# A two-layer hybrid decoder trunk: x loaded first, rotary angles and gate rows on GpSimd, six first-layer weight tiles stored split, split tiles brought back on two rings

## The chip, the cores and the metric

The kernel runs on one core of a Trainium2 chip. The core has a matrix engine (TensorE, PE in the profile), a vector engine (VectorE, DVE), an activation engine (ScalarE, ACT), a general engine (GpSimd, POOL), a queue engine that here does nothing but issue transfers (SyncE, SP), and 16 DMA engines. The metric is the time of one execution on the device, in microseconds (us).

## The reference, cut to what matters

```python
# S = 1024 tokens, D = 1024, 2 layers, everything float32
c_act = silu(c)
for l in range(2):
    mod = c_act @ ada_w[l] + ada_b[l]               # 6 rows of 1024: shift, scale, gate, twice
    h = rms_norm(x, g_pre_mix[l]) * (1 + scale_m) + shift_m
    proj = h @ w_in[l] + b_in[l]                    # 512 q | 128 k | 128 v | 512 u
    q, k = partial_rotary(q, positions), partial_rotary(k, positions)   # 16 of 64 dims
    attn_out = sliding_window_attention_with_sinks(q, k, v, sinks[l])   # window 128, 8 heads, 2 kv heads
    pool_out = causal_pool_mixer(u, pool_w[l], pool_scale[l])           # means over 2, 4, 8, 16 positions
    mix = concatenate([attn_out, pool_out]) @ w_out[l]
    x = x + gate_m * rms_norm(mix, g_post_mix[l])
    h = rms_norm(x, g_pre_ffn[l]) * (1 + scale_f) + shift_f
    f = (silu(h @ w_gate[l]) * (h @ w_up[l])) @ w_down[l]               # 1024 -> 2816 -> 1024
    x = x + gate_f * rms_norm(f, g_post_ffn[l])
```

## The kernel before, in words

**Three products for one.** Each float32 matrix is split into a rounded part `hi` and a rest `lo`. `split` does it: ScalarE copies with rounding (L223), VectorE subtracts (L224). A float32 product is then three matmuls on TensorE, hi·hi, hi·lo and lo·hi, all recorded at L285, nearly all 512 columns wide. Transposes stand at L290. Accumulators in PSUM are called `acc`, `msc` and `pv`.

**Halves and passes.** The 1024 tokens are worked on in two halves of 512 (`h` = 0 and 1). In each layer the first half goes through the q, k and v columns of `w_in` and the second half comes later; the u columns, attention, the pool mixer and the output projection follow, woven together so that TensorE always has something, then the gate, up and down products. So every piece of `w_in` is used twice, once for each half. `weight` loads a 128x512 piece into `raw` and splits it into one half of a `hi` tile and one half of a `lo` tile; `part` hands out these halves. There are three `hi` tiles and three `lo` tiles of 128x1024, each kind used in turn. A tile that comes round again may be written only when TensorE has done the last matmul that reads it.

**Tiles that are stored split.** `weight_once` is the helper around `weight` for the pieces of `w_in`. In layer 0 for the u columns, and in layer 1 for all pieces, it stores the split piece after its first use in a scratch tensor in HBM (`parted`, 128x1024, 512 KB: hi and lo side by side, two stores on SP, L253). At the second use it brings both halves back with one transfer into a whole `lo` tile (L247), and nothing is split again. For the q and kv pieces of layer 0 (`q0_0` to `kv7_0`) the raw piece is loaded and split a second time.

**The start.** SP issues `c_raw`, the five transfers of 72 rows that later become columns (`load_col_rows`, L396, tile `ar`), and then the first block of modulation weights (`cfa<-in_ada_w_dram`, L426, four transfers of 256 KB). ScalarE issues the four tiles of x (`fn`, 128x1024, 512 KB each, L183), and GpSimd the positions (L151). VectorE computes the rotary angles (`rotary_angles`, L195 to L212) from the positions, and casts the identity matrix (`ident`, L156) that every transpose needs. TensorE's first instruction is the transpose of the 72 rows (`cols_of`, L402); after it come the first modulation rows (`ada_first_row`, L448, 8 products of `c_act` with 256 columns, two records each), the first transposes of normalised x, and the second row. `stats` takes the squares of x on ScalarE (L614) and VectorE (L628); the reciprocal root stands in L344 to L351. For later blocks VectorE sums the modulation columns (L437, L439).

**Gate rows.** The modulation's gate rows are summed by VectorE elsewhere in the stream (L581), reduced by two matmuls with one row of output, and finished in `ada_gate`'s `close` by two VectorE instructions on 1x512 (L544, L545) before SP stores the row (L546). There are eight such half rows.

**The tail.** In the last down projection `ended` is called for each finished 128x512 tile: ScalarE squares it (L614), VectorE multiplies it by the gate in place (L1778), and `finish` forms the reciprocal root (L750 to L755), scales, adds the residual (L772) and stores the output (L775).

**What sets the order.** Every engine runs its own list of instructions in program order; the lists come from the order in which the code issues them and, for TensorE in part, from generators that are woven by estimated due times (`CLOSE`, `GAPS`, `LEADS` and the numbers that are yielded). SP issues transfers in the order of its list: a transfer whose destination is still in use stops all that stand behind it. Transfers signal through eight lanes that are used in turn, so a new transfer also waits for the eighth before it (in the lists: `DMAHW0` to `DMAHW7`, and `DMASW...` for those that GpSimd issues).

Of the kernel before, what the change touches and what calls it, by code (L numbers as in the profile page):

```python
# [68 lines left out]
def hybrid_decoder_kernel(  # L69
# [81 lines left out]
    nc.gpsimd.dma_start(pos_i, positions[0].rearrange("(t p) -> p t", p=P))  # L151
# [27 lines left out]
    nc.sync.dma_start(c_raw, c[0].rearrange("(p j) -> p j", j=KD))  # L179
    x0 = []  # L180
    for t in range(NT):
        x0.append(t_("fn", [P, D]))
        nc.scalar.dma_start(x0[t], x[0, t * P : (t + 1) * P, :])  # L183
# [10 lines left out]
    def rotary_angles():  # L194
        nc.vector.tensor_copy(pos_f, pos_i)  # L195
        for i in range(RH):
            nc.vector.tensor_scalar(ang[:, :, i], pos_f, float(inv_freq[i]), None, op0=ALU.mult)
        nc.vector.tensor_scalar(turns, ang, 1.0 / (2.0 * math.pi), None, op0=ALU.mult)
        nc.vector.tensor_scalar(turns, turns, ROUND_MAGIC, None, op0=ALU.add)
        nc.vector.tensor_scalar(turns, turns, ROUND_MAGIC, None, op0=ALU.subtract)  # L200
# [4 lines left out]
        nc.vector.tensor_scalar(up, ang, math.pi, -math.pi, op0=ALU.min, op1=ALU.max)  # L205
        nc.vector.tensor_scalar(sin_t[:, :, halves[0]], up, -1.0, None, op0=ALU.mult)
        nc.vector.tensor_tensor(turns, sin_t[:, :, halves[0]], up, op=ALU.max)
        for half in halves:
            nc.vector.tensor_scalar(cos_t[:, :, half], turns, -1.0, math.pi / 2.0, op0=ALU.mult, op1=ALU.add)
# [31 lines left out]
    parted = {}  # L241

    def weight_once(key, *srcs):

        if key in parted:
            both = part("lo", 1024)
            nc.sync.dma_start(both.bitcast(F32), parted.pop(key))  # L247
            return both[:, 0:512], both[:, 512:1024]
        hi, lo = weight(*srcs)
        if key[0] == "u" or key[-1] == "1":  # L250
            parted[key] = both = dr.tile([P, 1024], F32, tag=key, name="parted", bufs=1)
            for i, src in enumerate((hi, lo)):
                nc.sync.dma_start(both[:, i * 512 : (i + 1) * 512], src.bitcast(F32))  # L253
# [135 lines left out]
    def load_col_rows(l):  # L389
        rows = t_("ar", [P, 512])[:NROW, :P]  # L390
# [139 lines left out]
    def ada_gate(l, sub):  # L530
# [3 lines left out]
        def close(half, hi, lo):  # L534
# [9 lines left out]
            nc.vector.tensor_add(gb, bank[0:1, :], gb)  # L544
            nc.vector.tensor_mul(gb, gb, gg)  # L545
# [48 lines left out]
    CLOSE = 1.89  # L594
    GAPS = (0.71, 1.06)
# [162 lines left out]
    def finish(h, t, fn, ss, G, xt=None, ahead=None):  # L758
# [6 lines left out]
        for i in range(2):  # L765
# [5 lines left out]
            else:  # L771
                nc.vector.scalar_tensor_tensor(  # L772
                    fn[t][:, cs], fn[t][:, cs], rstd, xt[:, cs], op0=ALU.mult, op1=ALU.add
                )
            nc.sync.dma_start(out[0, h * T + rows.start : h * T + rows.stop, cs], fn[t][:, cs])  # L775
# [350 lines left out]
    LEADS = (0.9, 0.85, 0.21, 2.72, 1.2, 0.94)  # L1126
# [3 lines left out]
    def pool_mix(l, h, uts, cols, cat):  # L1130
# [14 lines left out]
        for g, w in enumerate(WINDOWS):  # L1145
# [22 lines left out]
            yield 1.7 if h else 2.82  # L1168
# [365 lines left out]
    rows0 = load_col_rows(0)  # L1534
# [40 lines left out]
    for b in range(NB0):  # L1575
# [24 lines left out]
        if 0 < b < NB0 - 1:  # L1600
            first_pieces(b + 1)
        if (k0 + nk) % 2 == 0:
# [5 lines left out]
    for l in range(DEPTH):  # L1608
# [29 lines left out]
        def gate_flow():  # L1638
# [4 lines left out]
            yield from ada_flow([two], [cats[1][1][:, i, :] for i in range(4)], 1.91)  # L1643

        gate = Chain(gate_flow())
        att = attention(0, qkvs[0], par["sink"], cats[0][0], 0.47, 3.23)
# [16 lines left out]
        pair = Chain(ada_flow(ada_pair(l, 1, par["cols"], par["abf"]), ring, 0.91))  # L1663
# [6 lines left out]
        def first_half():  # L1670
            for _ in post_norm(0, fn, ss, res0):
                yield 0.59
# [88 lines left out]
        def ended(name, t):  # L1761
# [13 lines left out]
            elif name == "p4":  # L1775
                square_sum(ss[1], t, 0, fn[1][t][:, 0:512])
                if not nxt:
                    nc.vector.tensor_mul(fn[1][t][:, 0:512], fn[1][t][:, 0:512], G[:, 0:512])  # L1778
                    finish(1, t, fn[1], ss[1], G, tail[t], aheads[t])
# [64 lines left out]
```

## Time and profile before

| | |
|---|---|
| time, median of 3 runs | 1867.78 us (1867.1 to 1868.0) |
| the profiled execution: its own time, its span | 1870.79 us, 1869.1 us |
| TensorE busy | 1835.1 us, 98% of the span |
| VectorE, ScalarE, GpSimd busy | 1501.5 us (80%), 919.7 us (49%), 100.3 us (5%) |
| moved by DMA | 363.84 MB, mean 195 GB/s |
| mean granted clock of TensorE | 0.997 |

The profiled execution is 3.0 us above the median of the runs without a profile, and its span lacks 1.7 us of its own time. A row of the timeline gives the start in us from the span's beginning, the time from the first instruction of a group to the end of its last, the engine (a q behind the name is that engine's issue of a transfer), the line, the operation, what is written from what, the number of instructions, and in brackets the idle time of the engine just before and what ended it.

### The profile page before, as it was taken

To read this page: it belongs to the slowest core of one execution; us is meant where nothing else is said; L and a number is where in the kernel's file an instruction comes from. 1 tells how busy PE (TensorE), PEld (TensorE's weight loads), DVE (VectorE), ACT (ScalarE), POOL (GpSimd) and SP (SyncE) were. 2 spreads that over 40 slices of the span, in tenths; PEclk is the share of its full clock that TensorE was granted. 3 is DMA by queue.
4 is the path that set the end of the run, shared out by engine and by line. 5 is a ranking of instruction groups with operands and counts; after the bars stand their busy time and mean duration, and the time that the engine had idled before them with its cause. 6 is when DMAs were issued, how large, how long until landed. Compare 5 with 4: busy or idle time off the path is not lost.

```text
span 1869.1 us, 25361 instructions
## 1 busy us (share of the span) xinstructions
PE 1835.1 (98%) x8662; PEld 1515.4 (81%) x8662; DVE 1501.5 (80%) x2492; ACT 919.7 (49%) x1757; POOL 100.3 (5%) x204
## 2 busy tenths in 40 slices
PE   7999999999999999999999999999999999999998
PEld 5888888888888888888887788888887887888886
DVE  7899885688888978879778788856878888877687
ACT  4885785562222223445648559755522222244452
POOL 0021130000000000000001202200000000000000
PEclk9999999999999999999999999999999999999999
DMA  9646744665456556844586676446646456574343
GB/s 341 201 141 215 259 147 143 208 215 181 167 188 218 183 180 225 298 147 133 194 302 202 213 233 217 155 135 209 220 157 207 162 200 229 176 270 142 113 146 114
DMA packets 237089, 363.84 MB, mean 195 GB/s; under 512 B 17912, under 2 KB 126344, under 8 KB 236960
## 3 DMA queue, kind: packets, MB, share of 16 engines
q1 hardware_dynamic: 236352, 360.13, 57.2%
q10 hardware_dynamic: 576, 2.10, 0.3%
q8 instruction: 68, 1.11, 0.2%
q14 instruction: 61, 0.50, 0.1%
q0 software_dynamic: 32, 0.00, 0.0%
HBM read 274.59 MB, written 87.57 MB: 194 GB/s over the span
## 4 chain that ended last, share of the span: by engine, by line
PE 83%; DVE 8%; DMA 4%; ACT 3%; issue 1%; SPq 1%; DVEq 0%; POOL 0%; ACTq 0%; POOLq 0%
PE acc L285 75%; PE msc L285 3%; PE msc L290 2%; PE pv L285 2%; DVE lo L224 1%; DMA raw<-in_w_up_dram 1%; DMA raw<-in_w_in_dram 1%; ACT hi L223 1%; DVE fn L1322 1%; SPq L426 0%; DVE ada L581 0%; DMA ar<-x 0%; DVE st L1026 0%; ACT sb L1034 0%; DVE raw L1337 0%
## 5 line engine op out<-in xcount | busy, mean ns | idle before, releaser
L223 ACT ACTIVATE hi<-raw 128x1024 fp32r<-128x1024 f32 (+2 forms) x360 | 315.6, 889 | 385.2 <-PE acc L285 243.6
L224 DVE TENSOR_TENSOR lo<-raw,hi 128x1024 fp32r<-128x1024 f32 (+2 forms) x360 | 363.0, 1016 | 115.9 <-ACT hi L223 110.7
L285 PE MATMUL acc<-t,hi 128*128 128x512 f32 x1408 | 432.1, 390 | 3.2 <-ACT hi L223 3.2
L285 PEld LDWEIGHTS acc<-t,hi 128*128 128x128 f32 x1408 | 263.6, 188 | 59.7 <-ACT hi L223 5.6
L285 PE MATMUL acc<-t,lo 128*128 128x512 f32 x704 | 271.9, 389 | 0.8 <-DVE lo L224 0.8
L285 PE MATMUL acc<-hT,hi 128*128 128x512 f32 x832 | 260.2, 394 | 0.0
L285 PE MATMUL acc<-hT,lo 128*128 128x512 f32 x608 | 213.4, 393 | 0.5 <-DVE lo L224 0.4
L285 PE MATMUL acc<-bh,hi 128*128 128x512 f32 x520 | 202.8, 390 | 0.0
L285 PE MATMUL acc<-bh,lo 128*128 128x512 f32 x520 | 202.4, 389 | 0.0
L1322 DVE TENSOR_TENSOR fn<-acc,fn 128x512 f32<-128x512 f32 x220 | 150.8, 686 | 33.7 <-PE acc L285 33.6
L285 PEld LDWEIGHTS acc<-hT,hi 128*128 128x128 f32 x832 | 151.8, 188 | 28.1
L285 PEld LDWEIGHTS acc<-t,lo 128*128 128x128 f32 x704 | 132.1, 188 | 30.0 <-DVE lo L224 2.4
L285 PEld LDWEIGHTS acc<-hT,lo 128*128 128x128 f32 x608 | 112.4, 188 | 25.8 <-DVE lo L224 1.3
L285 PE MATMUL acc<-ph,hi 128*128 128x512 f32 x328 | 126.5, 390 | 0.0
L1247 ACT ACTIVATE fn<-fn 128x512 f32<-128x512 f32 x44 | 27.9, 633 | 188.2 <-DVE fn L1322 188.2
L285 PEld LDWEIGHTS acc<-bh,lo 128*128 128x128 f32 x520 | 97.6, 188 | 20.4
L285 PEld LDWEIGHTS acc<-bh,hi 128*128 128x128 f32 x520 | 97.6, 188 | 20.2
L285 PE MATMUL acc<-b,hi 128*128 128x512 f32 x352 | 108.4, 389 | 0.0
L285 PE MATMUL acc<-lo,hT 128*128 128x512 f32 (+1 forms) x352 | 95.8, 349 | 3.9 <-DMA lo<-parted 2.9
L223 ACT ACTIVATE bh<-two_b 128x512 fp32r<-128x512 f32 x100 | 62.3, 623 | 71.2 <-PE acc L285 70.5
L285 PE MATMUL acc<-hi,hT 128*128 128x512 f32 (+1 forms) x320 | 88.8, 351 | 0.6 <-ACT hT L223 0.5
L285 PE MATMUL acc<-hi 128*128 128x512 f32 x224 | 87.6, 391 | 0.8 <-DVE fn L806 0.8
(320 smaller groups left out, 3235.3 us busy)
## 6 DMA issues: line engine op xcount, KB each, us to landing
raw<-in_w_gate_dram SPq DMA_DIRECT2D x44, 512.0 KB
raw<-in_w_up_dram SPq DMA_DIRECT2D x44, 512.0 KB
cfb<-in_ada_w_dram SPq DMA_DIRECT2D x80, 256.0 KB
raw<-keeps SPq DMA_DIRECT2D x40, 512.0 KB
keeps<-fn SPq DMA_DIRECT2D x66, 256.0 KB
ar<-in_ada_w_dram SPq DMA_DIRECT2D x64, 256.0 KB
two_b<-in_w_down_dram SPq DMA_DIRECT2D x30, 512.0 KB
lo<-parted SPq DMA_DIRECT2D x28, 512.0 KB
```

Of the source, the lines that this page charges most:

```text
L223: a = nc.scalar.activation(hi, src, AF.Copy)
L224: v = nc.vector.tensor_sub(lo, src, hi.bitcast(F32))
L285: return nc.tensor.matmul(dst, lhs, rhs, start=start, stop=stop)
L290: return nc.tensor.transpose(dst, src, eye_)
L1247: nc.scalar.activation(g, g, AF.Silu)
L1322: nc.vector.tensor_add(halves_of(dst)[m], bank, halves_of(src)[m])
```

## The change

**Start.** x is loaded first, from SP, with `c_raw` behind the first tile; the positions go to ScalarE's queue; the 72 rows go to the tile `ada`. The first modulation row is issued ahead of the transpose of the 72 rows. The rotary angles are computed by GpSimd (the fused multiply and add becomes two instructions, with `cos_t` as scratch), and the three instructions for the cosines are moved to VectorE's work in block 2 of the first pass.

**Split tiles.** Six q and kv pieces of layer 0 (`EARLY`) are also stored split, by GpSimd, and brought back at their second use. All returns now go alternately to a `hi` tile and a `lo` tile.

**Gate rows.** ScalarE copies the row out of PSUM, GpSimd adds and multiplies.

**Tail.** The multiplication by the gate writes into `fn[0][t]`, no longer in place, and `finish` reads from there.

**Numbers.** `CLOSE`, `GAPS`, `LEADS` and seven yielded numbers are other ones.

```diff
-    nc.gpsimd.dma_start(pos_i, positions[0].rearrange("(t p) -> p t", p=P))
+    nc.scalar.dma_start(pos_i, positions[0].rearrange("(t p) -> p t", p=P))
...
-    nc.sync.dma_start(c_raw, c[0].rearrange("(p j) -> p j", j=KD))
-    x0 = []
+    x0 = [t_("fn", [P, D]) for _ in range(NT)]
     for t in range(NT):
-        x0.append(t_("fn", [P, D]))
-        nc.scalar.dma_start(x0[t], x[0, t * P : (t + 1) * P, :])
+        nc.sync.dma_start(x0[t], x[0, t * P : (t + 1) * P, :])
+        if t == 0:
+            nc.sync.dma_start(c_raw, c[0].rearrange("(p j) -> p j", j=KD))
...
     def rotary_angles():
-        nc.vector.tensor_copy(pos_f, pos_i)
+        nc.gpsimd.tensor_copy(pos_f, pos_i)
         for i in range(RH):
-            nc.vector.tensor_scalar(ang[:, :, i], pos_f, float(inv_freq[i]), None, op0=ALU.mult)
+            nc.gpsimd.tensor_scalar(ang[:, :, i], pos_f, float(inv_freq[i]), None, op0=ALU.mult)
...
         for part in two_pi_parts():
-            nc.vector.scalar_tensor_tensor(ang, turns, -part, ang, op0=ALU.mult, op1=ALU.add)
+            nc.gpsimd.tensor_scalar(cos_t[:, :, 0:RH], turns, -part, None, op0=ALU.mult)
+            nc.gpsimd.tensor_add(ang, cos_t[:, :, 0:RH], ang)
...
+    def rotary_cosines():
+        halves = [sin_t[:, :, 0:RH], sin_t[:, :, RH:ROT]]
+        after(nc.vector.tensor_tensor(turns, *halves, op=ALU.max), recent["split"])
+        for half in (slice(0, RH), slice(RH, ROT)):
+            nc.vector.tensor_scalar(cos_t[:, :, half], turns, -1.0, math.pi / 2.0, op0=ALU.mult, op1=ALU.add)
...
+    EARLY = ("q4_0", "q5_0", "q6_0", "q7_0", "kv4_0", "kv6_0")
 
     def weight_once(key, *srcs):
 
         if key in parted:
-            both = part("lo", 1024)
+            recent["ring"] = "hi" if recent.get("ring") == "lo" else "lo"
+            both = part(recent["ring"], 1024)
             nc.sync.dma_start(both.bitcast(F32), parted.pop(key))
             return both[:, 0:512], both[:, 512:1024]
         hi, lo = weight(*srcs)
-        if key[0] == "u" or key[-1] == "1":
+        early = key in EARLY
+        if early or key[0] == "u" or key[-1] == "1":
             parted[key] = both = dr.tile([P, 1024], F32, tag=key, name="parted", bufs=1)
             for i, src in enumerate((hi, lo)):
-                nc.sync.dma_start(both[:, i * 512 : (i + 1) * 512], src.bitcast(F32))
+                (nc.gpsimd if early else nc.sync).dma_start(both[:, i * 512 : (i + 1) * 512], src.bitcast(F32))
         return hi, lo
...
-            nc.vector.tensor_add(gb, bank[0:1, :], gb)
-            nc.vector.tensor_mul(gb, gb, gg)
+            gr = t_("ph", [P, 512], F32R)[0:1].bitcast(F32)
+            nc.scalar.activation(gr, bank[0:1, :], AF.Copy)
+            nc.gpsimd.tensor_add(gb, gr, gb)
+            nc.gpsimd.tensor_mul(gb, gb, gg)
             nc.sync.dma_start(row[:, o], gb)
...
-    LEADS = (0.9, 0.85, 0.21, 2.72, 1.2, 0.94)
+    LEADS = (0.85, 0.85, 0.25, 2.72, 1.13, 1.11)
...
-    rows0 = load_col_rows(0)
+    rows0 = load_col_rows(0, "ada")
...
+    acc = ada_first_row(wss[0])
     par = layer_cols(0, rows0)
-    acc = ada_first_row(wss[0])
     rotary_angles()
...
+        if b == 2:
+            rotary_cosines()
...
                 if not nxt:
-                    nc.vector.tensor_mul(fn[1][t][:, 0:512], fn[1][t][:, 0:512], G[:, 0:512])
-                    finish(1, t, fn[1], ss[1], G, tail[t], aheads[t])
+                    nc.vector.tensor_mul(fn[0][t][:, 0:512], fn[1][t][:, 0:512], G[:, 0:512])
+                    finish(1, t, (fn[0][t], fn[1][t]), ss[1], G, tail[t], aheads[t])
```

Two places show how the lists of instructions move. The first is the start of VectorE's list. Before, the rotary chain (from L195, on the tiles `pos_f`, `pt`, `sin_t` and `cos_t`) stands ahead of the identity:

```order
L165 CAST picks<-pth 128x7
L195 CAST pos_f<-pos_i 128x8
L197 TENSOR_SCALAR pt<-pos_f 128x8 x8
L198 TENSOR_SCALAR pt<-pt 128x64
L199 TENSOR_SCALAR pt<-pt 128x64
L200 TENSOR_SCALAR pt<-pt 128x64
L202 SCALAR_TENSOR_TENSOR pt<-pt 128x64 x7
L205 TENSOR_SCALAR sin_t<-pt 128x8x8
L206 TENSOR_SCALAR sin_t<-sin_t 128x8x8
L207 TENSOR_TENSOR pt<-sin_t 128x64
L209 TENSOR_SCALAR cos_t<-pt 128x8x8 x2
L156 CAST ident<-G 128x128
```

Now the same engine goes from the small constants to the identity and to the squares of x (line 637 is line 628 of before):

```order
L163 MEMSET pth 128x7
L160 CAST ones_r<-pt 128x1
L164 MEMSET pth 128x1
L165 CAST picks<-pth 128x7
L156 CAST ident<-G 128x128
L209 TENSOR_SCALAR rcnt<-tpos 128x16 x4
L637 ISA pth,rs<-fn 128x512
L637 ISA rs 128x1
L210 RECIPROCAL rcnt<-rcnt 128x64
```

Nothing that waits for a transfer stands ahead of the identity any more. SP's list at the same place, before, with what each transfer waits for:

```order
L179 DMA c_raw<-in_c_dram 128x8
L396 DMA ar<-in_ada_b_dram 48x128
L396 DMA ar<-in_g_pre_mix_dram 8x128
L396 DMA ar<-in_g_pre_ffn_dram 8x128
L396 DMA ar<-in_pool_scale_dram 4x128
L396 DMA ar<-in_b_in_dram 4x128
L426 DMA cfa<-in_ada_w_dram 128x4x128 [waits DMAHW0_49]
L426 DMA cfa<-in_ada_w_dram 128x4x128 [waits DMAHW2_49]
L426 DMA cfa<-in_ada_w_dram 128x4x128 [waits DMAHW3_49]
L426 DMA cfa<-in_ada_w_dram 128x4x128 [waits DMAHW5_49]
L236 DMA raw<-in_w_in_dram 128x512 [waits DMAHW6_49]
```

And now, with x in the same list (L433 is L426 of before):

```order
L181 DMA fn<-in_x_dram 128x1024
L183 DMA c_raw<-in_c_dram 128x8
L181 DMA fn<-in_x_dram 128x1024 x3
L403 DMA ada<-in_ada_b_dram 48x128
L403 DMA ada<-in_g_pre_mix_dram 8x128
L403 DMA ada<-in_g_pre_ffn_dram 8x128 [waits DMAHW0_49]
L403 DMA ada<-in_pool_scale_dram 4x128 [waits DMAHW1_49]
L403 DMA ada<-in_b_in_dram 4x128 [waits DMAHW2_49]
L433 DMA cfa<-in_ada_w_dram 128x4x128 [waits DMAHW3_49]
L433 DMA cfa<-in_ada_w_dram 128x4x128 [waits DMAHW4_49]
L433 DMA cfa<-in_ada_w_dram 128x4x128 [waits DMAHW5_49]
```

All of x stands ahead of the rows and of `cfa`; the first three of the four `cfa` transfers now wait for the lanes of the second, third and fourth tile of x. The second place is the return of the split pieces in layer 1, on SP, near 1040 us of the trace; before, each goes to a `lo` tile, and waits until TensorE has done with it:

```order
L247 DMA lo<-parted 128x1024 [waits DMAHW4_49,PE_49]
L236 DMA raw<-in_w_out_dram 64x512 [waits DMAHW5_49]
L236 DMA raw<-in_w_out_dram 64x512 [waits DMAHW6_49]
L247 DMA lo<-parted 128x1024 [waits DMAHW7_49,PE_49]
L568 DMA cfb<-in_ada_w_dram 128x512 [waits DMAHW0_49,DVE_49]
L568 DMA cfb<-in_ada_w_dram 128x512 [waits DMAHW1_49,DVE_49]
L236 DMA raw<-in_w_out_dram 64x512 [waits DMAHW2_49]
L236 DMA raw<-in_w_out_dram 64x512 [waits DMAHW3_49]
L236 DMA raw<-in_w_out_dram 64x512 [waits DMAHW4_49]
L247 DMA lo<-parted 128x1024 [waits DMAHW5_49,PE_49]
```

and now the returns go to tiles of both kinds:

```order
L253 DMA hi<-parted 128x1024 [waits PE_49]
L240 DMA raw<-in_w_out_dram 64x512 [waits DMAHW5_49]
L253 DMA lo<-parted 128x1024 [waits DMAHW6_49,PE_49]
L577 DMA cfb<-in_ada_w_dram 128x512 [waits DMAHW7_49,DVE_49]
L253 DMA lo<-parted 128x1024 [waits DMAHW0_49,PE_49]
L577 DMA cfb<-in_ada_w_dram 128x512 [waits DMAHW1_49,DVE_49]
L240 DMA raw<-in_w_out_dram 64x512 [waits DMAHW2_49]
L240 DMA raw<-in_w_out_dram 64x512 [waits DMAHW3_49]
L240 DMA raw<-in_w_out_dram 64x512 [waits DMAHW4_49]
L253 DMA hi<-parted 128x1024 [waits DMAHW5_49,PE_49,Activation_49]
```

Six tiles instead of three take the returns, and each still waits for TensorE.

More of the change, by code (lines that the diff above doesn't have):

```diff
@@ L1642, in gate_flow @@
                 yield 0.5
[L1643 removed]
+            yield from ada_flow([two], [cats[1][1][:, i, :] for i in range(4)], 2.49)
         gate = Chain(gate_flow())
[L1646 removed]
+        att = attention(0, qkvs[0], par["sink"], cats[0][0], 0.55, 3.23)
         def dense():
```

31 lines of the change are left out of this document (14 added, 17 removed).

## The prediction

> **What bounds the kernel now.** I read the page's busy times and its chain first, then who waited for whom on TensorE, then the timeline around the longest of these waits, and last the table of stretches.
>
> ```profile
> span 1869.1 us, 25361 instructions
> PE 1835.1 (98%) x8662; PEld 1515.4 (81%) x8662; DVE 1501.5 (80%) x2492; ACT 919.7 (49%) x1757; POOL 100.3 (5%) x204
> ...
> PE 83%; DVE 8%; DMA 4%; ACT 3%; issue 1%; SPq 1%; DVEq 0%; POOL 0%; ACTq 0%; POOLq 0%
> ```
>
> TensorE is busy 98% of the span and carries 83% of the chain that ended last. The change leaves its products as they are, so only time in which TensorE waits, or runs at a lower clock, can be won. Its longest waits, with total, count and longest:
>
> ```profile
> PE msc L402 <- DVE ident L156: 11.8, 1, 11.8
> PE acc L285 <- ACT hi L223: 3.2, 4, 1.4
> PE acc L285 <- DMA lo<-parted: 2.9, 2, 1.6
> ```
>
> Apart from the start the largest is 3.2 us in four pieces, so the prize is small: the first instructions, the returns of split pieces, and the end. A difference of 0.2%, 3.7 us, is about what a measurement of this kernel can tell from no change.
>
> **The start.** The timeline, from the first loads to the point where TensorE runs on without a wait:
>
> ```profile
> 0.80 6.51 ACTq L183 DMA_DIRECT2D fn<-in_x_dram  x4
> 1.35 1.04 POOL L151 DMA_DIRECT2D pos_i<-in_positions_dram  x1 [0.34 <-issue]
> 4.59 3.09 SPq L426 DMA_DIRECT2D cfa<-in_ada_w_dram  x4
> 7.20 0.17 DVE L195 CAST pos_f<-pos_i 128x8 f32<-128x8 int32 x1 [5.71 <-DMA pos_i<-in_positions_dram]
> 7.35 1.28 ACT L184 ACT_TABLE_LOAD   x1 [7.35 <-DMA fn<-in_x_dram]
> 11.84 0.38 PE L402 MATMUL msc<-ident,ar 72*128 72x72 f32 x1 [11.84 <-DVE ident L156]
> 12.14 5.86 PE L448 MATMUL msc<-cfa,c_act 128*1 128x256 f32 x16
> 13.79 0.63 ACT L614 ACTIVATE junk<-fn 128x512 bf16<-128x512 f32 x1 [2.82 <-DMA fn<-in_x_dram]
> ...
> 26.56 0.63 ACT L223 ACTIVATE hi<-raw 128x512 fp32r<-128x512 f32 x1 [2.97 <-DMA raw<-in_w_in_dram]
> 27.10 0.76 ACT L667 ACTIVATE uT<-msc,colp 128x512 f32<-128x512 f32 x1
> ...
> 28.58 0.50 PE L285 MATMUL acc<-hi,hT 128*128 128x512 f32 x1 [0.55 <-ACT hT L223]
> ```
>
> VectorE gets the positions only at 7.20, works through the rotary chain, and makes the identity last, so TensorE starts at 11.84 and its row products at 12.14. The stretches give PE, PEld, DVE, ACT and POOL busy, then granted clock, DMA share and GB/s:
>
> ```profile
> 0.00:12.00 12.00, 0.17 (x1) 0.17 (x1) 4.80 (x34) 3.55 (x8) 3.29 (x16) 1.00 0.78 249
> 12.00:24.00 12.00, 11.87 (x45) 4.59 (x46) 9.04 (x36) 5.72 (x13) 0.00 (x0) 1.00 1.03 330
> 24.00:40.00 16.00, 15.45 (x91) 13.01 (x90) 14.60 (x28) 7.11 (x11) 0.00 (x0) 1.00 1.08 389
> ```
>
> The transfers are the second limit here: the DMA engines are full from 12 us to 40 us.
>
> With the change the row products come first and need `c_act` and half a block of `cfa`, no identity and no rotary chain. Ahead of them on one queue lie four tiles of x (2.10 MB) and 0.52 MB of `cfa`, 2.62 MB. At the 249 GB/s of the first stretch, idle time at its head included, they are there at 10.5 us; at the 389 GB/s of the third, counted from the first issue at 0.80, at 7.5 us. I take 10.0, nearest the first, since the head of the stretch stays: the row products start 2.1 us earlier (ends 1.6 and 4.6). ScalarE now loads two tables, 1.3 us more by the row at 7.35, but its squares can begin with the first tile, far before 13.79, so 10 us still covers that.
>
> What this is worth is decided at 28.58, where TensorE last waits: ScalarE waited 2.97 us for a raw piece before 26.56 and stood there with `uT` and `hT` behind it. That piece lies behind the same bytes as before. It comes earlier only by what the queues win at the head: 22% of 12 us is idle, 2.6 us, of which I give 0.5 to x being issued in one go; and x in an unmixed stream at 389 instead of 330 GB/s saves 2.10/0.330 − 2.10/0.389 = 1.0 us. So 1.5. In the new list of ScalarE `uT` stands ahead of that split instead of behind it, so its 0.76 no longer comes between piece and `hT`: 2.2 at most, 2.1 by TensorE's own start. I take **−1.9**. Ends: 0 (data no earlier) and −3.0 (also the 0.55 wait gone, and a little more).
>
> The rotary chain on GpSimd, some 27 small instructions, I cost at nothing: GpSimd is idle from 12 to 40 us, and the angles are first used after the first q rows of the pass are finished. The three cosine instructions go to VectorE in a stretch where TensorE doesn't wait: nothing.
>
> **The returns.** Around 1040 us:
>
> ```profile
> 1037.26 0.34 SPq L247 DMA_DIRECT2D lo<-parted  x1
> ...
> 1037.89 3.02 PE L285 MATMUL acc<-lo,hT 128*128 128x512 f32 x12
> ...
> 1040.94 0.34 SPq L247 DMA_DIRECT2D lo<-parted  x1
> ...
> 1042.23 0.98 PE L285 MATMUL acc<-lo,hT 128*128 128x512 f32 x3 [1.32 <-DMA lo<-parted]
> ...
> 1044.78 1.65 PE L285 MATMUL acc<-lo,hT 128*128 128x512 f32 x3 [1.57 <-DMA lo<-parted]
> ```
>
> Two returns are issued late, since each waits for a `lo` tile that TensorE frees late; 4.97 us (1037.26 to 1042.23) and 3.84 us (1040.94 to 1044.78) later TensorE begins on them. It waits 2.89 us, and then the clock drops; the stretch behind it:
>
> ```profile
> 1044.78:1051.50 6.72, 6.72 (x22) 5.49 (x23) 1.47 (x3) 3.57 (x7) 0.00 (x0) 0.54 0.46 127
> ```
>
> At a granted clock of 0.54, 6.72 us hold 3.6 us of work: 3.1 us more are lost, 6.0 in all. In the Trainium skill, "TensorE: Matmul & The Clock Gate", Part 1 on the clock gate, half rate follows an idle window of about 3.4 us; the two waits of 1.32 and 1.57 are shorter, by that rule the returns would be worth 2.9 and the sum would end at 1862.0. The row with 0.54 shows otherwise, and it decides.
>
> In TensorE's lists, 20 and 3 instructions stand between the one that frees the tile and the first that reads these two pieces, before. At 0.24 us for a 512-column matmul (twelve in 3.02 us, less 0.39 for the last: 2.63/11), and less for narrower ones, that is about 3.7 and 0.7 us. With two rings 36 and 43 stand there, 6.6 and 8.5 us, against 4.97 and 3.84 needed. No other return in the new lists has less. Both waits should go: **−6.0**. Ends: −6.5 (also small waits beside them) and 0 (below).
>
> **The six early pieces.** They take six splits out of the second q and kv pass of layer 0. One wait of that pass hangs on a split, and a split costs both engines:
>
> ```profile
> PE acc L285 <- DVE lo L224: 1.0, 1, 1.0
> ...
> L223 ACT ACTIVATE hi<-raw 128x512 fp32r<-128x512 f32 x48 | 30.1, 632 | 52.8 <-PE acc L285 36.1 <-issue 11.7 <-DMA raw<-keeps 1.9
> ...
> L224 DVE TENSOR_TENSOR lo<-raw,hi 128x512 fp32r<-128x512 f32 x48 | 33.2, 696 | 25.2 <-ACT hi L223 23.0 <-DMA raw<-in_w_up_dram 2.1
> ```
>
> The first row is that wait near 126 us. Six splits are 3.8 us of ScalarE and 4.2 of VectorE, all beside TensorE but for this 1.0 us: **−0.8** (ends −1.2 and 0). In return 3.1 MB are written near 42 to 58 us and 1.6 MB more are read back later:
>
> ```profile
> 42.00:58.00 16.00, 16.00 (x108) 14.64 (x108) 12.11 (x27) 14.21 (x33) 0.15 (x2) 1.00 0.65 237
> 58.00:66.00 8.00, 8.00 (x48) 7.12 (x47) 7.83 (x23) 3.36 (x6) 0.64 (x3) 1.00 0.68 230
> ```
>
> 3.1 MB at 389 GB/s are 8.1 us of all DMA engines; 35% of 16 us and 32% of 8 are free, 8.2 us, so they fit, just. Twelve issues at the 1.04 us of GpSimd's one transfer (row at 1.35) are 12.5 us of an engine that has 16 us free there. What waits is the first split of the u pieces, since it takes tiles that these stores read; the small u-side copies on GpSimd stand behind the stores too. I put **+0.4** on it; ends 0 and the rival below.
>
> **Gate rows.** Eight rows give up two VectorE instructions each:
>
> ```profile
> L544 DVE TENSOR_TENSOR ar<-msc,ar 1x512 f32<-1x512 f32 x8 | 5.4, 670 | 0.0
> ...
> L1098 POOL TENSOR_TENSOR sb<-qkv 128x128 f32<-128x128 f32 x14 | 8.3, 592 | 111.2 <-PE msc L290 74.4 <-DVE sb L1022 29.2 <-DVE lo L224 4.0
> ```
>
> GpSimd's nearest row is 0.59 us for 128 columns, so 512 cost between that and four times that. Two of them and ScalarE's copy (about a split's 0.63) replace 1.34 us: a row is stored 0.5 to 4 us later. SP waits for it with returns behind it, which now have 6.6 us or more against the 5.0 that one took; the upper end would eat that cover once. 0; ends −0.3 and +2.
>
> **The tail.**
>
> ```profile
> 1861.14 0.68 DVE L1417 TENSOR_TENSOR sb<-acc,sb 128x512 f32<-128x512 f32 x1
> 1861.92 0.63 ACT L614 ACTIVATE junk<-sb 128x512 bf16<-128x512 f32 x1 [2.92 <-DVE sb L1417]
> 1862.45 0.19 ACT L614 ACTIVATION_READ_ACCUMULATOR junk<-sb 128x1 f32 x1
> 1862.67 0.69 DVE L1778 TENSOR_TENSOR sb<-sb,G 128x512 f32<-128x512 f32 x1 [0.85 <-ACT junk L614]
> 1863.28 0.15 DVE L750 SCALAR_TENSOR_TENSOR rs<-ss,st 128x1 f32<-128x1 f32 x1
> ```
>
> The multiplication overwrites what ScalarE squares, so it waits 0.85 us. Written to another tile it runs beside the square; L750 then waits only for the accumulator, and starts near 1862.67 instead of 1863.28: **−0.6** (ends −0.7 and 0).
>
> **The numbers of the weave** move some products past others. TensorE's remaining waits are 1.4 us or less each, and I find no reason for a sign: 0, ends −1 and +2.
>
> **The sum**: −1.9 − 6.0 − 0.8 + 0.4 − 0.6 = −8.9. The profiled execution took 1870.79 us, 3.0 more than the median, and the difference is carried over unchanged: 1867.78 − 8.9 = **1858.9**.
>
> **The rivals.** *The start is bound by its data.* The full queues of 12 to 40 us speak for it: then −1.9 falls away, −7.0, 1860.8. Against it speaks the idle 22% at the head.
>
> *The returns move their wait instead of losing it.* The `hi` tiles also take the splits of everything else, and a split that waits for a return's tile stops ScalarE with all behind it. If the 6.0 us only change their place, −2.9 is left: 1864.9, no measurable change. TensorE's list, with 36 and 43 instructions of cover, speaks against it.
>
> *Slower: the stores on GpSimd hold the tiles.* The first u pieces' split is done by the row
>
> ```profile
> 58.40 0.33 SPq L253 DMA_DIRECT2D parted<-hi  x1
> ```
>
> and needs tiles that the early stores must have left. Suppose GpSimd gets its descriptors out only while VectorE is idle: that is 3.9 us of 42 to 58 and 0.2 of 58 to 66, against 12.5 needed. The last stores would go out past 66 us, and TensorE would stand for 10 us or more: 1858.9 + 10 and about 3 at half clock, 1872 or above. It decides against the change once the stores hold that split 6 us too long, since each microsecond of wait cost 2.1 at 1040 (6.0/2.89). The trace has one GpSimd transfer, 4 KB, under little VectorE work, and can't say. The Trainium skill has a reason for it: "SBUF — State Buffer", section "SBUF: two separate sides", says that descriptors of a transfer issued by GpSimd are starved while VectorE runs an instruction that takes both ports. No run here shows it yet.
>
> **How the numbers follow.** The forecast gets 0.62, with 1855.5 to 1862 for itself; the data-bound start 0.16; the moved wait 0.14; the held tiles 0.08. Faster by over 0.2% (under 1864.0): the first two and a small part of the third, 0.80. Within it: the rest of the third and a mild form of the last, 0.13. Slower: 0.07. The range takes in the first three to 1865; its low end is the sum of the lower ends of start, returns, pass and tail, −11.4, and 1 from the weave: 1855.4, so 1855.
>
> **What would show it.** In the changed profile TensorE's first row product near 10 us and its wait at 28.58 moved to about 26.7; no wait for a return of a split piece in layer 1 and a granted clock of 1.0 between 1030 and 1045; the wait near 126 us gone; GpSimd's stores all issued before 60 us; the last VectorE chain 0.6 us shorter behind the last matmul. Wrong it would be through a new wait of more than 3 us between 55 and 75 us, since that also costs clock, or a wait of ScalarE's splits on tiles that a return holds.

## The result and the profile after

The change made the kernel slower: 1884.57 us median (1881.86 to 1891.87, 5 runs) against 1868.0 (1867.1 to 1868.58, 5 runs), a ratio of 1.0095 with a 95% interval of 1.0073 to 1.0116. The forecast was 1858.9, range 1855 to 1865. The profiled execution took 1884.57 us, with a span of 1882.9.

The page's busy times and chain after the change:

```profile
PE 1837.4 (98%) x8662; PEld 1515.9 (81%) x8662; DVE 1487.1 (79%) x2449; ACT 923.5 (49%) x1760; POOL 137.5 (7%) x259
...
PE 75%; DVE 11%; DMA 7%; ACT 4%; issue 2%; SPq 1%; POOL 0%; DVEq 0%; POOLq 0%; ACTq 0%
```

TensorE has the same work, VectorE 14 us less, GpSimd 37 us more, and TensorE's share of the chain fell from 83% to 75%: VectorE, DMA and ScalarE hold the end more often. Who TensorE waited for:

```profile
PE msc L455 <- DMA cfa<-in_ada_w_dram: 12.2, 1, 12.2
PE acc L292 <- DVE lo L228: 6.8, 4, 2.4
PE acc L292 <- ACT hi L227: 4.8, 4, 2.6
PE msc L297 <- ACT sa L988: 3.2, 4, 1.6
...
PE acc L292 <- DMA lo<-parted: 0.5, 1, 0.5
```

The first wait has changed its cause and not its length: the identity is out of the way, and now the weights come at 12.2. The waits for returned pieces fell from 2.9 to 0.5. The waits for splits grew: for VectorE's half of them (L224 before, L228 now) from 2.2 to 6.8.

Both traces do nearly the same products in nearly the same order, so they can be laid over each other at equal amounts of TensorE work. How far the changed one is behind, in us, where it moves by much (the expectations call this the ledger):

| place (us of the trace after) | lag there | step |
|---|---|---|
| first products, 12.6 | +0.4 | |
| 25.3 | −0.6 | −1.0 |
| 37.4 to 92.5 | −0.2 to +1.9 | +2.1 |
| 102.7 to 115.0, a gate row of layer 0's mixing stage | +1.2 to +3.0 | +1.8 |
| to 136.4, end of the second q and kv pass | +2.2 | −0.7 |
| to 241.0 | +3.2 | +0.9 |
| to 548.8, first gate row of the up stage | +6.4 | +2.5 (last step) |
| to 662.5, second gate row of the up stage | +9.1 | +2.3 (last step) |
| 1042.0 to 1073.1, the returns | +10.4 to +3.8 | −6.7 |
| to 1445.9 | +7.9 | +3.1 (last step) |
| to 1582.2, second gate row, layer 1 | +11.1 | +4.1 (last step) |
| to the last products, 1875.0 | +14.9 | +3.0 (at 1846) |

So the returns gave what they should in this profile. The losses came at places that the prediction had put at nothing. Part of the last three steps is the clock. The stretches, in the columns of the prediction (the last three are granted clock, DMA share and GB/s):

```profile
1442.00:1446.00 4.00, 4.00 (x12) 2.69 (x11) 3.21 (x3) 1.05 (x2) 1.25 (x1) 0.57 0.15 39
1578.00:1582.00 4.00, 3.20 (x8) 2.53 (x9) 4.00 (x6) 0.20 (x1) 0.00 (x0) 0.58 0.61 220
1844.00:1848.00 4.00, 3.79 (x10) 3.04 (x11) 4.00 (x10) 2.20 (x6) 0.00 (x0) 0.61 0.00 0
```

Each lies behind waits of TensorE of 2.0 to 2.6 us, and each costs about 1.7 us of full clock, 5.1 of the 14.9 in all.

### The profile page after: what moved, and what is told of

Its sections match the earlier page's. It is cut to its first block, busy times and chain, and to the rows that moved or that the text cites. A ratio compares the mean times of both kernels' runs of the same rounds, so it can differ in the third digit from the quotient of the medians.

```text
span 1882.9 us, 25397 instructions
## 1 busy us (share of the span) xinstructions
PE 1837.4 (98%) x8662; PEld 1515.9 (81%) x8662; DVE 1487.1 (79%) x2449; ACT 923.5 (49%) x1760; POOL 137.5 (7%) x259
## 3 DMA queue, kind: packets, MB, share of 16 engines
q10 hardware_dynamic: 1040, 0.00, 0.0%
## 4 chain that ended last, share of the span: by engine, by line
PE 75%; DVE 11%; DMA 7%; ACT 4%; issue 2%; SPq 1%; POOL 0%; DVEq 0%; POOLq 0%; ACTq 0%
PE acc L292 66%; DMA raw<-in_w_up_dram 3%; PE msc L292 3%; PE msc L297 2%; PE pv L292 2%; DVE lo L228 2%; DVE fn L1331 1%; DMA ar<-x 1%; ACT hi L227 1%; DVE raw L1346 1%; DMA cfb<-in_ada_w_dram 1%; DVE raw L1347 1%; DVE fn L1257 1%; DMA raw<-in_w_in_dram 0%; DVE ada L590 0%
## 5 line engine op out<-in xcount | busy, mean ns | idle before, releaser
L227 ACT ACTIVATE hi<-raw 128x1024 fp32r<-128x1024 f32 (+2 forms) x354 | 311.5, 892 | 389.4 <-PE acc L292 247.7
L228 DVE TENSOR_TENSOR lo<-raw,hi 128x1024 fp32r<-128x1024 f32 (+2 forms) x354 | 358.4, 1019 | 127.8 <-ACT hi L227 125.2
L292 PE MATMUL acc<-hT,hi 128*128 128x512 f32 x928 | 286.8, 395 | 0.0
L292 PEld LDWEIGHTS acc<-hT,hi 128*128 128x128 f32 x928 | 169.0, 188 | 31.5
L292 PE MATMUL acc<-hT,lo 128*128 128x512 f32 x512 | 189.9, 393 | 0.1
L292 PEld LDWEIGHTS acc<-t,lo 128*128 128x128 f32 x704 | 132.8, 189 | 38.4 <-DVE lo L228 10.4
L292 PEld LDWEIGHTS acc<-hT,lo 128*128 128x128 f32 x512 | 94.7, 188 | 20.5 <-DVE fn L815 0.9
L292 PE MATMUL acc<-hi,hT 128*128 128x512 f32 (+1 forms) x400 | 100.1, 350 | 1.4 <-ACT hT L227 1.4
L292 PE MATMUL acc<-lo,hi 128*128 128x512 f32 x224 | 87.2, 389 | 0.0
```

The costliest lines, as they stand in the source:

```text
L227: a = nc.scalar.activation(hi, src, AF.Copy)
L228: v = nc.vector.tensor_sub(lo, src, hi.bitcast(F32))
L292: return nc.tensor.matmul(dst, lhs, rhs, start=start, stop=stop)
```

## The experiments

Each text says whether the edit is made to the kernel before, to the changed one, or to the changed one with the gate rows on VectorE. Each median stands beside runs of the kernel before on the same chip (medians 1867.7 to 1868.1). The name in brackets is that of the run.

**The gate rows back on VectorE (a_gate_dve).**

```diff
-            gr = t_("ph", [P, 512], F32R)[0:1].bitcast(F32)
-            nc.scalar.activation(gr, bank[0:1, :], AF.Copy)
-            nc.gpsimd.tensor_add(gb, gr, gb)
-            nc.gpsimd.tensor_mul(gb, gb, gg)
+            nc.vector.tensor_add(gb, bank[0:1, :], gb)
+            nc.vector.tensor_mul(gb, gb, gg)
```

> The changed kernel with one edit: the gate rows go back to two VectorE instructions reading PSUM. Theory G (the gate rows: GpSimd takes about 4 us for a row instead of VectorE's 1.3, and SP, which stores the row ahead of the next up-weight load, holds that load back): the four losses behind gate rows in the two gate and up stages (+3.4, +2.3, +3.1, +4.1 us in the ledger, 12.9 in all) go, so about 1884.6 - 12 = 1872, and the spread between runs shrinks. Rival E (GpSimd's stores of six early pieces disturb the rest): no change, 1882 to 1887.

Measured: 1868.36 (1865.66 to 1874.88), ratio 1.0003 (0.9992 to 1.0014). Sixteen microseconds come back by two lines; the whole rest of the change is worth nothing measurable.

**The same edit the other way, on the kernel before (b_gate_pool):**

> The kernel before with one edit: the gate rows as in the change (copy on ScalarE, add and multiply on GpSimd). Theory G: 1868 + 8 to 12, that is 1876 to 1880, with new waits of TensorE behind a late up-weight load in both gate and up stages. Rival E: 1868, no wait there.

Measured: 1890.26 (1888.10 to 1896.82), ratio 1.0121 (1.0103 to 1.0139): 22 us lost, more than expected. The gate rows on GpSimd alone make the kernel slower than the whole change does. Without the second ring the returns also suffer: in its profile, the slowest of the four executions, TensorE's two waits for them grew from 2.9 to 6.0 us, and the clock falls to half in five stretches, where the kernel before has one.

**Returns on two rings alone (b_rings):**

```diff
-            both = part("lo", 1024)
+            recent["ring"] = "hi" if recent.get("ring") == "lo" else "lo"
+            both = part(recent["ring"], 1024)
```

> The kernel before with one edit: returned pieces go alternately to a hi and a lo tile. Theory R (the step of the prediction): both waits near 1040 us go with the half clock behind them, 1868 - 6 = 1862. Rival: the wait only moves to splits that need the hi tiles, 1866 to 1868.

Measured: 1867.41 (1865.01 to 1868.80), ratio 0.9988 (0.9980 to 0.9997). In its profile the two waits near 1040 us are gone and 6.3 us with them, but the time is only 0.4 us shorter by the medians (1867.79 beside it) and about 2 by the ratio.

**No early pieces (a_noearly):**

```diff
-    EARLY = ("q4_0", "q5_0", "q6_0", "q7_0", "kv4_0", "kv6_0")
+    EARLY = ()
```

> The changed kernel with one edit: no early pieces, so no store on GpSimd; q and kv pieces of layer 0 are loaded and split twice again. Theory G: only the losses between 60 and 115 us go, about 2 us, and the wait near 126 us is back at 1 us: 1882 to 1885. Rival E: most of the loss goes, 1870 or less.

Measured: 1886.92 (1883.60 to 1889.46), ratio 1.0101 (1.0087 to 1.0116). Without them it is no faster; the stores on GpSimd are not the loss, and the losses between 60 and 115 us stayed, so my expectation for these was wrong.

**How the rows cost.** SP's list in the changed profile, near the first gate row of the up stage:

```profile
520.61 0.38 SPq L1314 DMA_DIRECT2D raw<-in_w_gate_dram  x1
524.24 0.23 SPq L555 DMA_DIRECT2D gate<-ar  x1
524.56 0.34 SPq L383 DMA_DIRECT2D ar<-in_ada_w_dram  x1
524.96 0.42 SPq L1314 DMA_DIRECT2D raw<-in_w_up_dram  x1
```

and GpSimd's two instructions for that row:

```profile
520.45 2.41 POOL L553 TENSOR_TENSOR ar<-ph,ar 1x512 f32<-1x512 f32 x1 [226.76 <-ACT ph L552]
522.94 1.27 POOL L554 TENSOR_TENSOR ar<-ar 1x512 f32<-1x512 f32 x1
```

GpSimd ends at 524.21 and the store goes out at 524.24. The up weights, which stood ahead of the store in the list before, stand behind it now, and go out 4.35 us after the gate weights. With the rows on VectorE (a_gate_dve), the same place:

```profile
519.30 0.38 SPq L1312 DMA_DIRECT2D raw<-in_w_gate_dram  x1
519.73 0.50 SPq L1312 DMA_DIRECT2D raw<-in_w_up_dram  x1
522.22 0.25 SPq L553 DMA_DIRECT2D gate<-ar  x1
```

0.43 us. So the change of the gate rows moved more than arithmetic: SP's own list came out in another order. At all four rows of the up stages the up weights stand ahead of the store here and behind it in the changed kernel. What the late loads do further on, in the changed profile:

```profile
535.35 1.23 DVE L1346 TENSOR_TENSOR raw<-raw 128x1024 f32<-128x1024 f32 x1 [3.03 <-DMA keepa<-sb]
...
541.29 1.22 DVE L228 TENSOR_TENSOR lo<-raw,hi 128x1024 fp32r<-128x1024 f32 x1
542.56 0.50 PE L292 MATMUL acc<-t,lo 128*128 128x512 f32 x1 [2.12 <-DVE lo L228]
```

VectorE combines raw weights with 3.03 us of idle time ahead of it (put down to a store issued just before; in a_gate_swq, below, the same instruction waits for `raw<-in_w_up_dram`), then works off what has gathered, the split comes late, and TensorE waits 2.12 us. Three versions were to separate SP's queue from the work itself.

**The store alone moved to GpSimd's queue (a_gate_swq):**

```diff
-            nc.sync.dma_start(row[:, o], gb)
+            nc.gpsimd.dma_start(row[:, o], gb)
```

> The changed kernel with one edit: the gate row is stored from GpSimd's own queue and not from SP, so GpSimd still takes its 4 us but no up-weight load stands behind the store. If SP's wait is the mechanism: 1884.6 - 12 = about 1871, like the version with the rows on VectorE (1868), with no wait of TensorE at the four places. If GpSimd's instructions themselves disturb VectorE or ScalarE: 1880 or more.

Measured: 1889.28 (1886.31 to 1891.18), ratio 1.0114 (1.0098 to 1.0130). By that expectation the queue was not the mechanism. Its profile, though:

```profile
522.07 0.38 SPq L1314 DMA_DIRECT2D raw<-in_w_gate_dram  x1
525.71 0.33 SPq L383 DMA_DIRECT2D ar<-in_ada_w_dram  x1
526.09 0.43 SPq L1314 DMA_DIRECT2D raw<-in_w_up_dram  x1
```

The up weights are 4.0 us behind again. The load ahead of them goes into an `ar` tile, and goes out when GpSimd's second instruction (524.40, 1.27 us) has ended.

**The row in the tile G, the store from GpSimd (a_gate_own):**

> The changed kernel with two edits: in the gate and up stages the gate row works in the tile G, which nothing else uses there, and every gate row is stored from GpSimd's queue. So GpSimd takes its 4 us as in the change, but SP has neither a store nor a load into an ar tile that waits for it ahead of an up-weight load. (The version with the store alone moved kept such a load: its ar tile was held by GpSimd, and the up weights were again issued 4 us behind the gate weights.) If SP's place in the queue is the mechanism: the four losses go, 1868 to 1871. If GpSimd's instructions or ScalarE's copy cost by themselves: 1880 or more.

Measured: 1884.79 (1884.19 to 1886.06), ratio 1.0091 (1.0077 to 1.0104). A third transfer had taken the place:

```profile
520.80 0.50 SPq L1317 DMA_DIRECT2D raw<-in_w_up_dram  x1
521.39 0.46 SPq L1323 DMA_DIRECT2D fn<-firsts  x1
527.38 0.25 SPq L549 DMA_DIRECT2D G<-in_ada_b_dram  x1
527.68 0.24 SPq L550 DMA_DIRECT2D G<-in_g_post_ffn_dram  x1
528.01 0.39 SPq L1317 DMA_DIRECT2D raw<-in_w_gate_dram  x1
```

The up weights are in time, but the next row's input waits for the single tile G, and holds the next pair of weights for 5.5 us.

**All transfers of the gate rows of the up stage on GpSimd's queue (a_gate_allq):**

```diff
+            eng = nc.gpsimd if sub else nc.sync
-            nc.sync.dma_start(gb, ada_b[l : l + 1, n0 : n0 + 512])
+            eng.dma_start(gb, ada_b[l : l + 1, n0 : n0 + 512])
...
-            nc.sync.dma_start(row[:, o], gb)
+            eng.dma_start(row[:, o], gb)
...
-        nc.sync.dma_start(G, gates[l, sub].to_broadcast([P, D]))
+        (nc.gpsimd if sub else nc.sync).dma_start(G, gates[l, sub].to_broadcast([P, D]))
```

> The changed kernel; in the gate and up stages every transfer of the gate rows (their two inputs, the store, the load of the finished gate) is issued by GpSimd, and the row works in the tile G. GpSimd still takes its 4 us, ScalarE still copies, but nothing on SP in these stages waits for either. In the two mends before, another transfer on SP waited for GpSimd's row instead (a load into an ar tile; the second row's input and the finished gate in G), and the up weights stayed 4 us late. If SP's queue is the mechanism: the losses near 545, 660 and 1580 go and 5 to 9 us come back, 1875 to 1879 (the mixing stage's rows keep their SP store). If it is GpSimd's or ScalarE's work itself: 1884.

Measured: 1876.99 (1870.29 to 1882.37), ratio 1.0043 (1.0028 to 1.0059): 7.6 us come back, as expected, and GpSimd takes as long as in the change. Against a_gate_own, where the rows of the up stage work in the same tile G, 7.8 us come back, and there the difference is only which queue the transfers are in. SP's list:

```profile
520.27 0.38 SPq L1318 DMA_DIRECT2D raw<-in_w_gate_dram  x1
520.71 0.50 SPq L1318 DMA_DIRECT2D raw<-in_w_up_dram  x1
...
526.14 0.37 SPq L1318 DMA_DIRECT2D raw<-in_w_gate_dram  x1
526.56 0.50 SPq L1318 DMA_DIRECT2D raw<-in_w_up_dram  x1
```

and GpSimd's row at the same time:

```profile
520.11 2.42 POOL L557 TENSOR_TENSOR G<-ph,G 1x512 f32<-1x512 f32 x1 [177.66 <-ACT ph L556]
522.61 1.28 POOL L558 TENSOR_TENSOR G<-G 1x512 f32<-1x512 f32 x1
```

In this execution, the fastest of its eight at 1870.29, the steps at the three gate rows that had cost 2.5, 2.3 and 4.1 us are each under 1 us. What the slower executions of this kernel lose was not seen in a profile and stays open; their mean granted clock is 0.996 to 0.998, that of the fastest 0.999.

**ScalarE's copy alone (e_gate_act)**, add and multiply on VectorE:

> The changed kernel with ScalarE's copy of the row kept, add and multiply on VectorE. If the copy on ScalarE costs by itself: well above the version without it (1868.4). If GpSimd's time is what counts: 1868 to 1870.

Measured: 1869.01 (1866.97 to 1873.02), ratio 1.0006 (0.9997 to 1.0014). The copy costs nothing measurable.

**Lateness alone (d_gate_delay)**, the row on VectorE and then `nc.gpsimd.tensor_copy(gb, gb)`:

> The changed kernel with the gate rows on VectorE and then one more copy of the row onto itself on GpSimd, about 1.3 us, ahead of SP's store: the work of the row is that of the fast version, only the store and the tile come 1.5 us later. If lateness of the row on SP is the mechanism: between 1868 and 1885, some 3 to 6 us above the fast version. If it is the 3 us of arithmetic on GpSimd: 1868 to 1869.

Measured: 1871.09 (1866.90 to 1873.63), ratio 1.0013 (1.0003 to 1.0023), 2.7 us above the version without it. The copy took 0.60 us and not 1.3, and the up weights kept their place ahead of the store. It points the expected way, but the intervals overlap, and it proves little.

**The start (c_pos_pool).** Positions back on GpSimd's queue, with the gate rows on VectorE:

```diff
-    nc.scalar.dma_start(pos_i, positions[0].rearrange("(t p) -> p t", p=P))
+    nc.gpsimd.dma_start(pos_i, positions[0].rearrange("(t p) -> p t", p=P))
```

> The version with gate rows on VectorE and one edit more: the positions are loaded from GpSimd's queue as before the change. In the changed kernel they go as 1040 packets of 4 bytes through ScalarE's queue, the DMA engines move 168 to 244 GB/s from 2 to 6 us, and SP's third row waits for that lane until 5.35. If that is what ate the start: cfa is issued near 6 instead of 7.60, the row products start near 10.5 instead of 12.2, and the time falls by 1 to 2 us to about 1867. If the queue of x ahead of cfa is what counts: start at 12, no change, 1868.

Measured: 1868.22 (1864.07 to 1873.41), ratio 1.0003 (0.9992 to 1.0013), row products at 12.35. The queue of the positions is not what holds the start; the order of x and `cfa` is left, and c_nostart below bears it out.

**Rotary and row order changed, transfers as before (b_ident):**

> The kernel before with the rotary angles on GpSimd and the row products ahead of the transpose; all transfers stay where they were (x from ScalarE's queue, positions from GpSimd's). If the start was held by the rotary chain and only the new order of transfers ate the gain: row products near 10 us, first q product 2 us earlier, 1866. If the later data bound the start anyway: row products earlier but the product at 28.6 unmoved, 1867.7.

Measured: 1867.08 (1863.70 to 1870.98), ratio 0.9997 (0.9987 to 1.0006). Its first product:

```profile
9.72 6.24 PE L452 MATMUL msc<-cfa,c_act 128*1 128x256 f32 x16 [9.72 <-DMA cfa<-in_ada_w_dram]
```

In the profile it is 2.4 us ahead of before at 37 us, in the median not measurably.

**x and positions from the old queues, with early pieces, new numbers and VectorE rows (c_nostart):**

> The version with gate rows on VectorE, with x and the positions loaded from the queues of before. Beside the last one it has the six early pieces and the new numbers. If the new order of the transfers at the start costs 1 to 2 us: 1866 to 1867, the row products near 10 us. If not: 1868.

Measured: 1864.87 (1861.89 to 1868.31), ratio 0.9985 (0.9976 to 0.9994), row products at 9.84: 3.5 us below the same version with x first.

**The weave's numbers of before (c_oldnums):**

> The version with gate rows on VectorE and the weave's numbers of the kernel before (CLOSE, GAPS, LEADS, the yielded ones). In the ledger that version loses 1.4 us near 225 to 240 us and 1.3 near 1150, the same place of both layers. If the numbers cause it: both gone, 1868.4 - 2.5 = about 1866. If not: 1868.

Measured: 1873.24 (1870.40 to 1875.66), ratio 1.0029 (1.0018 to 1.0040), against 1868.36 with the new numbers. A miss: the new numbers don't cost 2.5 us, they give 4.9 together with the early pieces; with the old ones 4.3 us are lost between 102 and 140 us, where its profile has a wait of 2.57 us for a returned piece (until 129.93) and a granted clock of 0.57 from 129 to 137 us.

**The kernel before, a second profile (before_2):**

> The kernel before, unchanged, for a second profile. If the half clock behind the two waits near 1040 us comes in every execution: 6 us lost there again, and about 1870 in the profiled run. If it came by chance in the one profile that the prediction read: the two waits of 1.3 and 1.6 us without the half clock, 3 us lost, and about 1867.5.

Measured: 1871.06 in the profiled run, the stop near 1040 us there again, about 1 us smaller: two waits of 2.42 and 1.05 us, then a granted clock of 0.76 from 1046 to 1053 us. Both profiled executions of this kernel are 3 us above its median; the profiled one of b_rings (1866.98) is not above its own.

**The best of the parts (b_best):** the kernel before with two rings, the tail, rotary on GpSimd and the row products first, all transfers of the start as before.

> The kernel before with the parts that cost nothing elsewhere: two rings, the tail's second tile, rotary on GpSimd with the row products first, transfers of the start as before. Rings -0.4 to -2, tail -0.6, start 0 to -2: 1864 to 1867.

Measured: 1863.72 (1861.48 to 1867.12), ratio 0.9976 (0.9965 to 0.9987): 4.2 us below the kernel before, and the fastest version of this study.

## Why the prediction was wrong, step by step

**Gate rows: the step that failed.** The prediction put them at "0; ends −0.3 and +2", because "SP waits for it with returns behind it, which now have 6.6 us or more". The prediction's price of the arithmetic was about right (a copy, then 2.41 and 1.27 us at the first row of the up stage, for 1.34). The cover was wrong. Returns stand behind the row in the mixing stages only. In the up stages the 512 KB of up weights stand behind it, and the new list of SP, which was at hand, shows the store ahead of them where it stood behind them before. Four of the eight rows were never looked up. Moving the rows back is worth 16 us of the 16.6 lost.

Of these 16, in the profiles, 2.5, 2.3 and 4.1 us lie at three of the four rows of the up stages, where SP's queue is shown as the mechanism by a_gate_allq; 1.7 of the 4.1 are the half clock behind the wait. In the mixing stages 1.8 and 0.6 us lie at one row each; there another mechanism shows, below. The steps near 1446 (+3.1) and 1846 us (+3.0) hold 1.7 us of half clock each; a_gate_dve and a_gate_allq have neither the steps nor the half clock there. But what made TensorE wait there is not traced to the rows: it stood idle from 1438.07 to 1440.62, and that stage's first row began on GpSimd only at 1444.75. Both waits follow transfers that landed later than before. That stays open. So does the wider spread between executions, though whether the clock falls behind a wait differs, and must add to it: behind the waits of 2.12 and 2.07 us at the rows of layer 0 it stayed whole.

**The start: −1.9 forecast, about 0 found.** "I take 10.0, nearest the first" failed; it was 12.20. All of x now lies ahead of `cfa`, and `cfa` waits for the lanes of x (SP's waits in the first 12 us: total, count, longest):

```profile
SPq L433 <- DMA fn<-in_x_dram: 3.0, 3, 1.2
```

```profile
7.60 3.54 SPq L433 DMA_DIRECT2D cfa<-in_ada_w_dram  x4
...
12.20 1.01 PE L455 MATMUL msc<-cfa,c_act 128*1 128x256 f32 x2 [12.20 <-DMA cfa<-in_ada_w_dram]
```

Before, `cfa` was issued at 4.59. I counted bytes and not the wait for a free lane, although the order showed it. The other half of the step was right: without the rotary chain the products start at 9.72 (b_ident). The wait that was to move from 28.58 to about 26.7 stands at 28.79 and is 1.38 us long. The rival "the start is bound by its data" had the size right, but not the reason, the full queues of 12 to 40 us: with the old order of the transfers a lead of 2.3 us is still there at 92 us of b_ident's profile. The new order costs more than the start: the lag that grows between 37 and 92 us stays with the rows on VectorE, about 1.8 us in a_gate_dve, and is 0.4 in c_nostart.

**The returns: −6.0 forecast, −6.7 in the profile, −0.4 to −2 in the time.** The granted clock after the change is whole at this place:

```profile
1040.00:1050.00 10.00, 10.00 (x54) 8.47 (x54) 9.83 (x24) 7.00 (x22) 3.61 (x7) 1.00 0.92 287
```

The mechanism was right: the waits went, and the clock stayed whole. The size was read from one profiled execution that was itself 3.0 us above the median, a difference that the prediction "carried over unchanged". The half clock in it, 3.1 us, does not come every time. b_ident has the returns of before and the same two waits, 1.50 and 1.10 us, and behind the second the clock is whole:

```profile
1044.33:1051.50 7.17, 7.17 (x40) 6.11 (x41) 4.04 (x9) 4.70 (x9) 1.38 (x3) 1.00 0.55 174
```

The runs beside the experiments point the same way. Of 91 runs of the kernel before on four chips, 31 have a mean granted clock of 0.997 or less, as the profiled one has, and took 1870.0 us on average; the other 60, with 0.998 or more, took 1867.4. So the prediction read one of the slower executions, and the median holds only part of the 3.1 us. Where the clock fell in the runs without a profile is not recorded, so this is inferred. A second part of the gap may be a moved wait or scatter: against the first profile of before, b_rings loses 3.8 us between 136 and 1030 us, and before_2, with nothing changed, loses 2.2 there.

**The early pieces: −0.8 + 0.4 forecast.** a_noearly is 2.4 us slower than the change, with overlapping ranges: no harm, and perhaps more than I gave. But the wait near 126 us that they were to remove is not in a_noearly either, so the reason for the −0.8 is not shown. The slower rival, that GpSimd's stores hold the tiles, did not happen: the first went out at 45.79, the last here, and no engine's wait between 42 and 80 us is put down to one of them:

```profile
58.99 0.54 POOL L260 DMA_DIRECT2D parted<-lo  x1 [0.24 <-DVE rs L631]
```

A slower kernel is what came, but the chance of 0.07 that the prediction gave to it belonged to this mechanism, which was not the one.

**The tail: −0.6 forecast, −0.6 found.** VectorE's last chain:

```profile
1875.40 0.69 DVE L1426 TENSOR_TENSOR sb<-acc,sb 128x512 f32<-128x512 f32 x1
1876.13 0.69 DVE L1789 TENSOR_TENSOR fn<-sb,G 128x512 f32<-128x512 f32 x1
...
1878.82 0.75 DVE L781 SCALAR_TENSOR_TENSOR sb<-sb,rs,hT 128x512 f32<-128x512 f32 x1
```

From the start of the first to the end of the last it takes 4.17 us, where it took 4.76 before (1861.14 to 1865.90).

**The numbers: 0 forecast.** Beside the other parts, early pieces included, they give 4.9 us (c_oldnums); alone they were not measured.

## What to carry to other kernels

When work moves to a slower engine, list for every place in the program what stands behind the instruction that waits for the result, on the queue that waits, and compare the old list with the new one there. Here a small row that was done 4 us late made the weights behind it on the queue 4 us late, and moving the store aside only handed the wait to the next transfer that needed the same tile. A gain that rests on one profiled execution should be checked against how that execution stands to the runs without a profile, in time and in mean granted clock.

## What the runs showed of the hardware

GpSimd and VectorE got into each other's way in the mixing stage, which I had not expected at all. In the changed profile, GpSimd's row:

```profile
107.67 1.57 POOL L553 TENSOR_TENSOR ar<-ph,ar 1x512 f32<-1x512 f32 x1 [0.44 <-ACT ph L552]
109.31 1.27 POOL L554 TENSOR_TENSOR ar<-ar 1x512 f32<-1x512 f32 x1
```

and VectorE at the same time:

```profile
108.00 1.42 DVE L949 TENSOR_TENSOR qkv<-qkv,cos_t 128x160 f32<-128x160 f32 x1
109.35 1.79 DVE L1165 SCALAR_TENSOR_TENSOR pt<-pt,uT 128x512 f32<-128x512 f32 x1
```

Two VectorE instructions that read two inputs each took 1.42 and 1.79 us here; their medians over the same profile:

```profile
L949 DVE TENSOR_TENSOR qkv<-qkv,cos_t x16: 307/314/1416, 67.9 to 1161.6; 128x160 f32<-128x160 f32 x16
...
L1165 DVE SCALAR_TENSOR_TENSOR pt<-pt,uT x16: 659/679/1790, 100.1 to 1185.8; 128x512 f32<-128x512 f32 x16
```

0.31 and 0.68 us. Each ends 0.2 to 0.6 us after the GpSimd instruction that it met (these end at 109.24 and 110.58), and the two together lose 2.2 us, near the 1.8 that TensorE loses there. ScalarE then waits 1.83 us for VectorE, and TensorE 1.6 us for ScalarE; neither wait is in a_gate_dve. The step is in every profile of the changed kernel with rows on GpSimd in that stage. In b_gate_pool, whose lists are in another order, the row meets other instructions: the step is missing there, and GpSimd's multiply took 1.72 us. The Trainium skill, "SBUF — State Buffer", section "SBUF: two separate sides", describes a port pair that the two engines share and that whichever comes first holds for its whole instruction; the trace agrees with that. GpSimd's own time for the add ran from 1.31 to 2.91 us over the eight rows, which fits the same lock from its side.

The positions, 1024 elements of 4 bytes each taken singly, made 1040 packets on ScalarE's queue and only 32 on GpSimd's. c_pos_pool, which moves them back, is no faster.

The clock behind a wait fell to half in some cases and not in others. It fell behind waits of 2.56 and 2.36 us, and behind pairs of 1.20 and 0.83, and of 1.32 and 1.57 us; it stayed whole behind single waits of 2.12 and 2.07 us and behind the pair of 1.50 and 1.10 us. So the length of the waits alone does not tell, in these runs, whether the half clock follows, and a gain that counts on it is an average at best.
